# DSA's cost entry 40.0 to 74.0 in the emission mix of a two-layer decoder kernel

## Chip, core and metric

The kernel runs on one core of a Trainium2 chip. The metric is the device time of one execution in microseconds (us). Engines are named as in the profile: PE is TensorE (matmuls), DVE VectorE, ACT ScalarE, POOL GpSimd, SP SyncE.

## What is computed

Two decoder layers on 512 tokens of width 1024. Each layer normalises the input, projects it, runs four mixers of width 256 side by side (HGRN2, DSA, NSA, mLSTM), projects their joined output back, adds a cross-attention over 256 memory rows, and ends in a feed-forward block. Only the index branch of DSA matters closely here:

```python
topk = min(DSA_TOPK_MAX, l_ // 4)                     # 128
def block(bi):                                        # 128 queries at a time
    ...
    rel = jax.nn.relu(jnp.einsum('bthd,bsd->bhts', iqb, ik))   # 8 index heads
    # weighted sum over the heads, causal mask, then the 128 best keys of each query;
    # attention of that query runs over these keys alone
```

So for each block of 128 queries (tb = 0 to 3) there are eight score products, a weighted sum, and a choice of the 128 largest keys. Block 0 needs no choice.

## The kernel before

**Stages.** Each layer has a first stage (DSA's index branch, NSA, mLSTM and the projections that feed them, `weave` at L1535), a second stage (HGRN2, called hg, DSA's attention, output projection, cross-attention) and the feed-forward block. In time: first and second stage of layer 1 lie in 0 to 523 us, feed-forward to 872, layer 2's stages to 1390, its feed-forward to the end.

**What sets the order.** The program is one static instruction list for each engine, and an engine works its list in order. Generators emit work and `yield` a cost after each piece; `mix` takes the generator whose emitted cost, divided by its total in the table COST (L200), is smallest. What was emitted earlier has precedence in the scheduler that then lays out the lists. Weight projections are emitted early and with high precedence through `first()`.

**The index branch.** `dsa` (L607) yields 4.0, then for tb = 1, 2, 3 eight times 0.7 from `index` and sixteen times 0.4 + 0.25 tb from `select`: 64 in all. `index(tb)` makes eight score matmuls (L644), evicts them on ACT (`rel`, L646) and adds them into `iacc` on DVE (L649 to L653). `select(tb)` runs 16 rounds on DVE, each a MAX8 (L661) and a MATCH_REPLACE8 with its MATCH_VALUE_LOAD (L662), and then writes the mask (`dmask`, L665). The width of a round is 128 (tb + 1): 256, 384, 512 columns.

**What stands behind it.** `hg_space` (L737) follows `dsa` in the same chain and closes the index branch's pool; `hg_in` (L743), last of the other chain, waits in emission until that is done, since the tiles `h_v` and `h_g` take that pool's place. `h_v` is a projection with the tokens on the partitions: 48 matmuls (L304 to L306, 128x256) for two blocks, into two PSUM banks `acc`, evicted on ACT at L450. Two more blocks follow, then h_g and the output projection. These weight matmuls need nothing from the mixers and fill PE while it would wait; they are called filler here.

**Names in the first stage.** mLSTM works head after head: 12 matmuls L1013 into the bank `mb`, the four evictions `m_p` (L1021, DVE), 20 matmuls L1030 (into `mb` again), then a normalisation `m_den` (L1034 on, DVE). L539, L517, L519, L458 and L570 are NSA's attention, L1126 its compressed branch. L678 to L688 prepare DSA's keys, L1246 transposes mLSTM's output, L821 are products of hg.

```python
def mix(self, *parts):
    parts = [[g, total, 0.0] for g, total in parts]
    while parts:
        p = min(parts, key=lambda p: p[2] / p[1])
        try:
            c = next(p[0]); p[2] += c
            yield c
```

```python
self.weave((self.chain(self.dsa(pd, pk), self.hg_space(index, right)), COST["dsa"]),
           (self.chain(self.nsa_in(pn), ...), COST["two"]))
```

Of the kernel before, what the change touches and what calls it, by code (L numbers as in the profile page):

```python
# [196 lines left out]
RAWS = 6  # L197

OUT_K = ((4, 5, 6, 7), (2, 3), (0, 1))
COST = {"dsa": 40.0, "nsa": 140.0, "ml": 41.0, "in": 78.0, "mlin": 100.0, "two": 225.0, "attn": 49.42, "hg": 92.2, "out": 21.47, "ahead": 1834.58}  # L200


class Kernel:
# [41 lines left out]
    def first(self):  # L245

        return ExitStack() if self.starting else self.tc.high_priority(offset=int(COST["ahead"]))

# [1248 lines left out]
    def run(self):  # L1497
        nc = self.nc
        late = ExitStack()
        for l in range(DEPTH):  # L1500
# [31 lines left out]
            for tb in range(TB):  # L1532
                with self.first():
                    nc.scalar.activation(self.d_idx[:, tb], acc[tb], AF.Copy, scale=self.rcol[:, tb:tb + 1])
            self.weave((self.chain(self.dsa(pd, pk), self.hg_space(index, right)), COST["dsa"]),  # L1535
                       (self.chain(self.nsa_in(pn),
                                   self.mix((self.nsa(pn), COST["nsa"]),
                                            (self.chain(self.ml_in(pm),
                                                        self.mix((self.ml(pm), COST["ml"]),
                                                                 (self.chain(self.ml_in2(pm), self.dsa_in2(pk), self.hg_in()), COST["in"]))),  # L1540
                                             COST["mlin"]))),
                        COST["two"]))
# [48 lines left out]
```

## Time and profile before

| what | value |
|---|---|
| time, median of 3 runs | 1744.96 us (1742.71 to 1750.66) |
| profiled execution | 1746.31 us, of which the profile's span is 1744.5 us |
| PE busy | 1660.6 us, 95% of the span |
| DVE busy | 917.5 us, 53% |
| POOL busy | 785.8 us, 45% |
| ACT busy | 721.2 us, 41% |
| mean granted TensorE clock | 0.93 of 2.4 GHz |

Busy shares are averages over stages. Matmuls overlap and their ends are modelled, so a PE that is busy all the time can still work at half of its clock: the granted clock must be read beside the busy time.

### The profile page before, as it was taken

What the parts mean: (1) busy time and instruction counts of PE and PEld (TensorE: products, weight loads), DVE (VectorE), ACT (ScalarE), POOL (GpSimd) and SP (SyncE); (2) the same over time, 40 slices, a digit from 0 to 9 for tenths busy, and PEclk for the clock granted to TensorE, in tenths of its full rate; (3) what the DMA queues carried; (4) which work ended last, traced back from release to release, by engine and by line L of the source; (5) the groups of instructions that cost most, each with busy time, mean ns of one, the idle gap of its engine ahead of it and who ended that gap; (6) DMA issues with size and microseconds to landing.
All of it is one profiled execution on the core that took longest, in us unless ns stands there. A gap on an engine that the chain in (4) does not pass through costs nothing.

```text
span 1744.5 us, 25169 instructions
## 1 busy us (share of the span) xinstructions
PE 1660.6 (95%) x9262; PEld 1377.2 (79%) x9262; DVE 917.5 (53%) x1760; ACT 721.2 (41%) x1525; POOL 785.8 (45%) x698
## 2 busy tenths in 40 slices
PE   7889996999899999999998899989998999999999
PEld 7868774878788888888897687779786888888887
DVE  5685578756764430443227935796658544214420
ACT  5455532245553322333345644413566533223321
POOL 6653332346714444444446523233565244444442
PEclk9989985699999999999999899856998999999999
DMA  5233111021503333333233312010232133333332
GB/s 167 80 98 84 55 39 62 23 69 46 161 13 98 97 88 101 96 97 95 87 106 86 113 51 69 25 55 25 80 94 83 43 91 94 89 101 97 92 102 66
DMA packets 83259, 140.40 MB, mean 80 GB/s; under 512 B 9528, under 2 KB 24632, under 8 KB 83136
## 3 DMA queue, kind: packets, MB, share of 16 engines
q1 hardware_dynamic: 80784, 133.81, 26.1%
q10 hardware_dynamic: 2032, 3.94, 0.7%
q8 instruction: 73, 1.20, 0.3%
q0 software_dynamic: 320, 1.05, 0.2%
q14 instruction: 50, 0.41, 0.1%
HBM read 134.55 MB, written 4.21 MB: 80 GB/s over the span
## 4 chain that ended last, share of the span: by engine, by line
PE 79%; DVE 12%; issue 3%; ACT 2%; DMA 2%; POOL 2%; SPq 0%; ACTq 0%; POOLq 0%; DVEq 0%
PE acc L294 13%; PE acc L295 12%; PE acc L296 12%; PE sc L295 5%; PE sc L296 5%; PE sc L294 5%; PE hb L821 3%; PE acc L304 3%; PE acc L305 3%; PE acc L306 2%; PE sc L517 2%; PE o L539 2%; PE mb L1030 2%; PE tp L458 1%; DMA wr<-in_wst 1%
## 5 line engine op out<-in xcount | busy, mean ns | idle before, releaser
L286 POOL TENSOR_TENSOR wl<-wr,wh 128x512 fp32r<-128x512 f32 (+5 forms) x504 | 629.7, 1257 | 736.6 <-ACT wh L285 717.8
L285 ACT ACTIVATE wh<-wr 128x512 fp32r<-128x512 f32 (+5 forms) x504 | 298.2, 597 | 505.8 <-PE acc L295 195.9
L294 PE MATMUL acc<-xh,wh 128*128 128x512 f32 (+1 forms) x704 | 274.8, 392 | 2.4 <-DVE xT L431 2.3
L296 PE MATMUL acc<-xh,wl 128*128 128x512 f32 (+1 forms) x704 | 273.7, 389 | 0.8 <-POOL wl L286 0.8
L295 PE MATMUL acc<-xl,wh 128*128 128x512 f32 (+1 forms) x704 | 274.0, 389 | 0.0
L431 DVE TENSOR_TENSOR xT<-acc,xT 128x512 f32<-128x512 f32 (+1 forms) x112 | 68.2, 612 | 231.4 <-PE acc L296 231.2
L294 PEld LDWEIGHTS acc<-xh,wh 128*128 128x128 f32 x704 | 132.9, 189 | 32.4 <-DVE xT L431 1.9
L296 PEld LDWEIGHTS acc<-xh,wl 128*128 128x128 f32 x704 | 133.1, 189 | 28.1 <-POOL wl L286 2.1
L295 PEld LDWEIGHTS acc<-xl,wh 128*128 128x128 f32 x704 | 133.2, 189 | 27.0 <-issue 0.4
L295 PE MATMUL sc<-xl,wh 128*128 128x512 f32 x352 | 139.6, 397 | 0.0
L304 PE MATMUL acc<-wh,xh 128*128 128x256 f32 (+2 forms) x480 | 139.0, 291 | 0.3 <-DVE xT L431 0.3
L296 PE MATMUL sc<-xh,wl 128*128 128x512 f32 x352 | 139.0, 395 | 0.0
L295 PE MATMUL acc<-f_gl,wh 128*128 128x512 f32 x352 | 138.3, 395 | 0.0
L294 PE MATMUL acc<-f_gh,wh 128*128 128x512 f32 x352 | 138.2, 395 | 0.0
L296 PE MATMUL acc<-f_gh,wl 128*128 128x512 f32 x352 | 138.2, 394 | 0.0
L294 PE MATMUL sc<-xh,wh 128*128 128x512 f32 x352 | 138.1, 393 | 0.0
L305 PE MATMUL acc<-wl,xh 128*128 128x256 f32 (+2 forms) x480 | 137.9, 289 | 0.0
L306 PE MATMUL acc<-wh,xl 128*128 128x256 f32 (+2 forms) x480 | 137.1, 287 | 0.0
L1450 DVE SCALAR_TENSOR_TENSOR f_b<-sc,R 128x512 f32<-128x512 f32 x44 | 30.4, 690 | 127.7 <-PE sc L296 127.7
L304 PEld LDWEIGHTS acc<-wh,xh 128*128 128x128 f32 x480 | 91.6, 191 | 3.0 <-issue 1.2
L305 PEld LDWEIGHTS acc<-wl,xh 128*128 128x128 f32 x480 | 91.7, 191 | 1.5 <-issue 0.5
L306 PEld LDWEIGHTS acc<-wh,xl 128*128 128x128 f32 x480 | 91.7, 191 | 0.2 <-issue 0.2
(405 smaller groups left out, 3151.9 us busy)
## 6 DMA issues: line engine op xcount, KB each, us to landing
wr<-in_wst SPq DMA_DIRECT2D x384, 256.0 KB, 2.6
wr<-in_wst SPq DMA_DIRECT2D x48, 128.0 KB, 2.2
wr<-in_wst SPq DMA_DIRECT2D x32, 192.0 KB, 2.4
wr<-in_wst SPq DMA_DIRECT2D x16, 262.0 KB, 2.7
wr<-in_wst SPq DMA_DIRECT2D x16, 148.0 KB, 2.4
wr<-in_wst SPq DMA_DIRECT2D x8, 264.0 KB, 2.8
m_Mb<-m_dram ACTq DMA_DIRECT2D x8, 256.0 KB, 3.6
xT<-in_xT SPq DMA_DIRECT2D x8, 256.0 KB, 4.5
```

Of the source, the lines that this page charges most:

```text
L285: nc.scalar.activation(hi, raw, AF.Copy)
L286: nc.gpsimd.tensor_tensor(lo, raw, hi.bitcast(FT), op=OP.subtract)
L294: self.nc.tensor.matmul(acc, wh, xh, start=(j == 0), stop=False)
L295: self.nc.tensor.matmul(acc, wh, xl, start=False, stop=False)
L296: self.nc.tensor.matmul(acc, wl, xh, start=False, stop=(j == n - 1))
L304: self.nc.tensor.matmul(acc, xh[:, s], wh, start=(first and j == 0), stop=False)
L305: self.nc.tensor.matmul(acc, xh[:, s], wl, start=False, stop=False)
L306: self.nc.tensor.matmul(acc, xl[:, s], wh, start=False, stop=(last and j == n - 1))
L431: self.nc.vector.tensor_add(self.xT[c][:, cols], acc, self.xT[c][:, cols])
L517: nc.tensor.matmul(sc[:, e], q[j][:, h0 + e], job["kst"][:, :n], start=(j == 0), stop=False, skip_group_check=True)
L539: nc.tensor.matmul(o[64 * e:64 * e + 64, hp], job["v"](sb), job["pT"][2 * hp + e][:, sb * 128:sb * 128 + 128], start=(sb == 0), stop=(sb = ...
L821: nc.tensor.matmul(sc[s0:s1, b + t0:b + t1], kk[po:po + 64, b + s0:b + s1], qq[po:po + 64, b + t0:b + t1], start=True, stop=True)
```

## The change

One number of the table COST is another; no generator, instruction or tile is added or removed.

```diff
-COST = {"dsa": 40.0, "nsa": 140.0, "ml": 41.0, ..., "two": 225.0, ...}
+COST = {"dsa": 74.0, "nsa": 140.0, "ml": 41.0, ..., "two": 225.0, ...}
```

The yields of `dsa` sum to 64. With 40 its progress passes 1 before its end, and it reaches 64/40 = 1.60: the rest of `mix`, whose progress ends at about 1, is emitted to its end before the last index block and its choice. With 74 its end lies at 64/74 = 0.87, so 13% of the other parts' list is emitted after it.

The DVE list in the first layer, where the choice for tb = 3 starts (`m_2942` and `m_2244` are the eight maxima of a round, `mo_106` mLSTM's output, `kv` DSA's keys, `m_p` mLSTM's evictions). Before:

```order
L1042 TENSOR_REDUCE m_den<-m_sq 128x4
L661 MAX m_2942<-iacc 128x8
L312 TENSOR_SCALAR rs_ms<-m_den 128x4
L662 MATCH_REPLACE iacc<-m_2942,iacc 128x512
L312 TENSOR_SCALAR rs_ms<-dt 128x4
L661 MAX m_2942<-iacc 128x8
L316 TENSOR_TENSOR mo_106<-mo_106,m_den 128x4x64
L662 MATCH_REPLACE iacc<-m_2942,iacc 128x512
L316 TENSOR_TENSOR mo_106<-mo_106,m_tok 128x4x64
L661 MAX m_2942<-iacc 128x8
L316 TENSOR_TENSOR kv<-dt,d_st_3273 128x512
```

After:

```order
L1021 SCALAR_TENSOR_TENSOR m_p_2862<-mb,m_d 128x512
L653 SCALAR_TENSOR_TENSOR iacc<-rel,d_idx,iacc 128x512
L661 MAX m_2244<-iacc 128x8
L316 TENSOR_TENSOR mo_105<-o,spread 128x2x128
L521 TENSOR_REDUCE stat<-sc 128x1
L662 MATCH_REPLACE iacc<-m_2244,iacc 128x512
L1021 SCALAR_TENSOR_TENSOR m_p_2871<-mb,m_d 128x384
L661 MAX m_2244<-iacc 128x8
L1021 SCALAR_TENSOR_TENSOR m_p_2934<-mb,m_d 128x256
L662 MATCH_REPLACE iacc<-m_2244,iacc 128x512
L1021 SCALAR_TENSOR_TENSOR m_p_2968<-mb,m_d 128x128
L661 MAX m_2244<-iacc 128x8
```

The 16 rounds stood behind mLSTM's last head, among the preparation of keys and hg. They now stand among the evictions of mLSTM's last two heads.

The ACT list around the eviction of the first two blocks of `h_v` (`qh` and `P` belong to DSA's attention, `m_d` and `m_sq` to mLSTM, `ckvsq` to DSA's keys). Before:

```order
L525 ACTIVATE P,stat<-sc,stat 128x256 x2
L338 ACTIVATE sq<-d_q 128x256
L490 ACTIVATE qh<-dt 128x512
L450 ACTIVATE h_v<-acc,r_2765 128x256 x2
L1278 ACTIVATE memacc<-memT 128x256
L450 ACTIVATE h_v<-acc,r_2765 128x256
```

After:

```order
L1019 ACTIVATE m_d<-m_Mb,m_cols 128x128
L678 ACTIVATE ckvsq<-d_ckv 128x512
L1017 ACTIVATE m_d<-m_Md,m_cols 128x128
L450 ACTIVATE h_v<-acc,r_2873 128x256 x2
L1041 ACTIVATE m_sq<-mo_106 128x256
L1278 ACTIVATE memacc<-memT 128x256
L450 ACTIVATE h_v<-acc,r_2873 128x256
```

The eviction stood behind two blocks of DSA's attention; it now stands before the last normalisation of mLSTM.

The PE list in the first layer, where the last index scores stand (`iqs` are the index queries, `PT`, `n_tok`, `n_kst` belong to NSA's attention). Before:

```order
L458 MATMUL dt<-kc,iqs 96x128 x4
L1013 MATMUL mb<-m_hi_2645,m_hi_2697 128x256
L1013 MATMUL mb<-m_lo,m_hi_2697 128x256
L1013 MATMUL mb<-m_hi_2645,m_lo 128x256
L458 MATMUL dt<-kc,iqs 96x128 x4
L1013 MATMUL mb<-m_hi_2645,m_hi_2697 128x128
L1013 MATMUL mb<-m_lo,m_hi_2697 128x128
L1013 MATMUL mb<-m_hi_2645,m_lo 128x128
L644 MATMUL dt<-ikT,iqT 128x512
```

After:

```order
L306 MATMUL acc<-wh,xl 128x256
L458 MATMUL tp<-kc,P 128x128 x4
L539 MATMUL o<-PT,n_tok 64x128
L517 MATMUL sc<-n_kst_846,qh 128x512
L517 MATMUL sc<-n_kst_846,ql 128x512
L519 LDWEIGHTS identb
L519 MATMUL sc<-trib,identb 128x128
L1013 MATMUL mb<-m_hi_2749,m_lo 128x512
L644 MATMUL dt<-ikT,iqT 128x512
L539 MATMUL o<-PT,n_tok 64x128 x7
```

The eight L644 of tb = 3 stood behind the last weight matmul of the stage, between mLSTM's matmuls. They now lie spread over the weight matmuls and NSA's attention; the eighth, shown here, comes after most of them. The second layer's lists move in the same way.

## Rows read from the trace of the kernel before

**Rows 1.** The page's second part: granted clock in 40 slices.
```profile
PEclk9989985699999999999999899856998999999999
```

**Rows 2.** Windows of layer 1; busy us and instructions by engine, clock, DMA.
```profile
core 0: us, PE busy (x) PEld busy (x) DVE busy (x) ACT busy (x) POOL busy (x), PEclk, DMA share, GB/s
...
100.00:130.00 30.00, 22.42 (x139) 18.06 (x140) 28.09 (x65) 17.07 (x44) 14.85 (x14) 0.72 0.30 89
...
210.00:247.00 37.00, 36.78 (x241) 29.45 (x239) 32.91 (x77) 13.46 (x26) 12.99 (x10) 1.00 0.20 53
...
430.00:470.00 40.00, 37.10 (x213) 31.10 (x212) 30.60 (x42) 24.86 (x53) 29.80 (x31) 1.00 0.51 154
470.00:523.00 53.00, 47.77 (x348) 40.45 (x348) 37.53 (x83) 31.11 (x78) 12.28 (x11) 0.94 0.12 37
```

**Rows 3.** Windows, same columns: from keys' preparation to the next filler, layers 1 and 2.
```profile
280.40:334.90 54.50, 39.57 (x177) 34.16 (x177) 52.53 (x132) 10.34 (x28) 20.18 (x29) 0.50 0.15 50
...
1144.10:1203.20 59.10, 53.85 (x253) 47.62 (x253) 58.20 (x142) 7.77 (x23) 22.73 (x36) 0.50 0.12 41
```

**Rows 4.** Windows of 10 us inside and behind the layer 1 stretch.
```profile
260.00:270.00 10.00, 9.08 (x24) 5.63 (x24) 6.33 (x16) 5.04 (x12) 1.02 (x1) 0.50 0.00 0
...
280.00:290.00 10.00, 2.08 (x8) 1.78 (x8) 9.97 (x29) 0.62 (x2) 4.47 (x11) 0.50 0.61 202
...
340.00:350.00 10.00, 10.00 (x85) 9.41 (x85) 0.18 (x1) 5.47 (x13) 5.08 (x4) 1.00 0.38 107
```

**Rows 5.** Timeline of PE: start, duration, line, operation, [idle before, releaser].
```profile
247.64 0.50 PE L1013 MATMUL mb<-m_hi,m_hi 64*128 64x512 f32 x1 [0.86 <-ACT m_hi L980]
...
272.11 4.53 PE L1030 MATMUL mb<-m_v,m_p 128*128 128x65 f32 x20
...
278.53 1.09 PE L1246 MATMUL tp<-kc,mo 128*128 128x128 f32 x4
...
334.86 0.58 PE L304 MATMUL acc<-wh,xh 128*128 128x256 f32 x1
...
1111.89 0.49 PE L1013 MATMUL mb<-m_hi,m_hi 64*128 64x512 f32 x1 [0.71 <-ACT m_hi L980]
...
1203.19 0.58 PE L304 MATMUL acc<-wh,xh 128*128 128x256 f32 x1
```

**Rows 6.** Timeline of DVE: mLSTM's last two heads.
```profile
249.86 0.68 DVE L1021 SCALAR_TENSOR_TENSOR m_p<-mb,m_d 128x512 f32<-128x512 f32 x1
...
262.15 0.16 DVE L1034 COPY m_den<-mb 128x4 f32<-128x4 f32 x1 [2.95 <-PE mb L1030]
...
265.81 0.69 DVE L1021 SCALAR_TENSOR_TENSOR m_p<-mb,m_d 128x512 f32<-128x512 f32 x1 [0.15 <-PE mb L1013]
...
271.77 0.28 DVE L1021 SCALAR_TENSOR_TENSOR m_p<-mb,m_d 128x128 f32<-128x128 f32 x1
```

**Rows 7.** Timeline of DVE: one round at 512 columns, and the last mask.
```profile
284.45 0.68 DVE L661 MAX8 m<-iacc 128x8 f32<-128x512 f32 x1
...
285.96 0.69 DVE L661 MAX8 m<-iacc 128x8 f32<-128x512 f32 x1
...
331.88 0.42 DVE L665 TENSOR_SCALAR dmask<-iacc 128x512 bf16<-128x512 f32 x1
```

**Rows 8.** Groups by line on PE in 247 to 279: busy us, mean ns | idle before.
```profile
L644 PE MATMUL dt<-ikT,iqT 96*128 96x512 f32 x8 | 6.3, 788 | 0.7 <-ACT rel L646 0.7
L458 PE MATMUL dt<-kc,iqs 128*96 128x128 f32 x8 | 2.2, 427 | 0.0
```

**Rows 9.** Timeline of ACT: eviction of the first two blocks of h_v.
```profile
332.44 0.83 ACT L450 ACTIVATE h_v<-acc,r 128x256 f32<-128x256 f32 x2
```

**Rows 10.** Timeline of DVE: one round at 256 columns (tb = 1).
```profile
126.15 0.43 DVE L661 MAX8 m<-iacc 128x8 f32<-128x256 f32 x1
...
127.13 0.43 DVE L661 MAX8 m<-iacc 128x8 f32<-128x256 f32 x1
```

More of the change, by code (lines that the diff above doesn't have):

```diff
@@ L199 @@
 OUT_K = ((4, 5, 6, 7), (2, 3), (0, 1))
-COST = {"dsa": 40.0, "nsa": 140.0, "ml": 41.0, "in": 78.0, "mlin": 100.0, "two": 225.0, "attn": 49.42, "hg": 92.2, "out": 21.47, "ahead": 1834.58}
+COST = {"dsa": 74.0, "nsa": 140.0, "ml": 41.0, "in": 78.0, "mlin": 100.0, "two": 225.0, "attn": 49.42, "hg": 92.2, "out": 21.47, "ahead": 1834.58}
 class Kernel:
```

## Prediction

> **What bounds the kernel now.** I read the granted clock in slices first, because PE is busy nearly everywhere and its busy share hides where it is slow. The clock is at full speed except in two places, one in each layer [rows 1]. Windows then show what these places are. In layer 1 the clock stands at 0.50, that is 1.2 of 2.4 GHz, from about 250 us on, and is 1.00 again in 340 to 350 [rows 4]. PE's timeline gives the ends: its last weight matmuls are over when mLSTM's next head starts at 247.64, and the next filler starts at 334.86; in layer 2 these are 1111.89 and 1203.19 [rows 5]. So each layer has a hole of some 87 to 91 us.
>
> The hole has two parts. First come mLSTM's last two heads, a chain that goes back and forth between PE and DVE, until L1246 at 278.53 [rows 5, 6]. Then DVE bounds: in 280.4 to 334.9 it is busy 52.53 of 54.5 us, in layer 2 58.20 of 59.1 [rows 3], with the 16 rounds of tb = 3 among the preparation of hg and of DSA's attention; at its worst PE has 2.08 us of work in 10 [rows 4]. It ends with the last mask at 331.88 [rows 7] and the eviction of `h_v` at 332.44 [rows 9], which frees the two banks that the filler needs. This eviction waits by its place in ACT's list, behind DSA's attention, not for anything of its own. The feed-forward blocks, two fifths of the span, run at full clock [rows 1] and are not touched.
>
> **What the change moves, layer 1.** No work is added; I price when the filler resumes (T) and how much PE work of the old hole is then still to be done.
>
> Start of the hole. The eight L644 and eight transposes of tb = 3 come out of the hole (6.3 + 2.2 us there, at half clock [rows 8]) and lie among dense matmuls, where I price them at half of that: 4.2 us. The rounds of tb = 1 and 2 stand 25 and about 50 places earlier in DVE's list. At 100 to 130 DVE is busy 28.09 of 30 us already and PE idles 7.6 us [rows 2]; rounds put ahead of what PE waits for there cost it time. The trace of before cannot show how much. Bounds are 0 (the later stretch 210 to 247 shows PE busy 36.78 of 37 us while the rounds of tb = 2 run on a DVE busy 32.91 [rows 2], so rounds can be hidden) and 10, the idle time there now and a third more. I take 5, nearer to the DVE-bound row, since the moved rounds come towards that stretch. The hole so starts at 247.6 + 4.2 + 5 = 256.8.
>
> Length of the hole. In DVE's new list the rounds lie among the last two heads. A round at 512 columns takes 1.51 us from MAX8 to MAX8 [rows 7]; 16 make 24. Step by step: the third head needs 12.3 us from its first `m_p` to its `m_den` (249.86 to 262.15 [rows 6]), and the five rounds put in there (7.5 us) fit into DVE's idle time beside it. Up to the fourth head's first `m_p` the chain took 3.7 us (262.15 to 265.81), now with three rounds in the same queue: 3.7 + 4.5 = 8.2. Through its four `m_p` it took 6.0 (265.81 to 271.77), with three and a half rounds, 5.3 us, between: 9, between 6.0 and 11.3. Then L1030, 4.5 us from 272.11, and L681 with L1246, some 3 us until 279.6 [rows 5]: 7.5. Sum 12.3 + 8.2 + 9 + 7.5 = 37. The last four rounds and the mask run beside this end. `h_v` is evicted by then, as it stands behind the last `m_d`, and the filler starts at T = 256.8 + 37 = 293.8 instead of 334.9: 41.1 us earlier.
>
> What is late next. In the old hole PE did hg and DSA attention work in 280.4 to 334.9, 39.57 us busy at clock 0.50 [rows 3]. In the new order that comes after T, mixed with filler, and I price it at full clock: 19.8 us. What is left is 41.1 - 19.8 = 21.3 us.
>
> **Layer 2** by the same steps: the hole starts 4.2 + 5 later than 1111.9, T = 1111.9 + 9.2 + 37 = 1158.1, which is 45.1 before 1203.2; the work to be done later is 53.85/2 = 26.9; left 18.2. Together 39.5 us.
>
> **What takes some of it back.** The filler (144 matmuls for the rest of `h_v` and for h_g, then the output projection) is used up while hg's chain and DSA's attention still run, and at the end of the second stage PE then waits for them. Now, 430 to 523 has 8.1 us of PE idle time [rows 2]. I bound the added wait by 0 and 12 us in each layer and take 5, somewhat over half of what is lost there now, so 10 for both.
>
> Sum: 39.5 - 10 = 29.5 us. The profiled execution took 1746.3 (span 1744.5 and 1.8 around it), which gives 1716.8; that execution stands 1.3 above the median of the runs, so I name 1716.
>
> **The clock in the new hole.** In 260 to 270 PE shows 9.08 of 10 us busy and still the granted clock is 0.50 [rows 4]; it comes back only in the filler. So I price the new hole at half clock, as the heads' rows are. The Trainium skill (TensorE: Matmul & The Clock Gate, section Why this matters for your kernels) says that idle gaps between bursts of matmuls bring the clock back to half rate. The trace agrees in the fall at 250, and by it the order after, which puts NSA's attention and the scores among dense matmuls, might keep the clock up to the end of the heads; that is rival A.
>
> **Rivals.** A, the clock holds, or is lost late. PE's part of the chain is then half as long: L1030's 4.5 us and about 7 us of the third head's 12.3 shrink, T comes 5.6 us earlier in each layer, and with the queue's loss at the front at 0 another 5: 21 us more, 1695. For it speaks that NSA's attention, at full clock before 247, now stands beside the third head; against it that rows of a nearly busy PE stay at 0.50 [rows 4].
>
> B, the rounds do not overlap the heads. If DVE's order makes each wait for the other, the hole is 32 us of heads (247.6 to 279.6) and 24 of rounds, 56 in place of 37. That takes 19 from each layer: 39.5 - 38 - up to 10, about 1745 to 1755, no change. For it: DVE and PE each work in order, and a head's eviction now waits behind up to two rounds. Against it: the rounds need nothing from PE once `iacc` is summed.
>
> C, slower: the earlier rounds of tb = 1 and 2 hold up the front. Place: DVE's queue at 100 to 150 and 970 to 1010, ahead of NSA's scores and mLSTM's `m_p`. Price: a round at 256 columns takes 0.98 us [rows 10], one at 384 about 1.25, halfway to the 1.51 of 512; 16 of each are 36 us in a layer, and if PE waits for all of them, with 5 already counted, the loss is 62 us: 1779. The change turns slower from about 20 us of front loss in each layer on. For it: PE stands at clock 0.72 in 100 to 130 for want of DVE [rows 2]. Against it: the same rounds are hidden in 210 to 247.
>
> D, the change has no effect, if `h_v` were held by the last mask as now. Its new place in ACT's list speaks against it; then T would be about 296 anyway.
>
> **How the numbers follow.** Forecast with its bounds 1700 to 1735: 0.56. A, about 1695: 0.13. B and D, 1736 to 1755: 0.17. C, over 1755, centre 1779: 0.14. The range that should hold 8 in 10 reaches from 1692 (A with a little more) to 1750 (most of B); C stays outside. A measurement here tells about 0.5%, 8.7 us, from no change: faster by more holds for the forecast, A and a small part of B, 0.71; within it 0.15; slower 0.14.
>
> **What would show it.** Right: clock 0.50 from about 257 to 295 and from 1121 to 1160 and not until 335 and 1203; the first `h_v` eviction at about 285 to 294; the last mask near 295. The front's loss: mLSTM's last two heads start at 257 rather than 252 (no loss) or over 270 (C). The tail: PE idle time of 13 us rather than 8 before the feed-forward, which itself starts near 507. It would be wrong first if the rounds and the heads' evictions queue up on DVE (mask near 313: B), or if filler resumes early but PE falls to half clock again in hg's levels.

## The result, and where the time went

The changed kernel takes 1701.0 us (1697.2 to 1706.9, 4 runs) against 1744.3 for the kernel before: ratio 0.9748, 95% interval [0.9708, 0.9788], 43 us less. The forecast was 1716, 29 us less. So the sign and the place of the gain were forecast, and the gain is half as large again as the sum. Not all of it came by the forecast's way: the run with 66 below gains 29 us although it leaves the sixteen rounds of tb = 3 behind the heads.

The feed-forward block starts after everything that the change moves. Its first and last evictions (L1450) show what each layer gained; the view is the line's own, kernel before and kernel after, with the first and last start:

```profile
L1450 DVE SCALAR_TENSOR_TENSOR f_b<-sc,R x44: 678/691/692, 531.9 to 1679.2; 128x512 f32<-128x512 f32 x44
```
```profile
L1450 DVE SCALAR_TENSOR_TENSOR f_b<-sc,R x44: 680/691/692, 510.2 to 1636.4; 128x512 f32<-128x512 f32 x44
```

Layer 1 gains 21.7 us, both together 42.8, so layer 2 gains 21.1. The page after, its second part (granted clock in 40 slices), answers to [rows 1]: the two slices at 5 and 6 in each layer have become one at 7 (255 to 298 and 1106 to 1149 us; the other 7, at 936, is the front of layer 2, which had 8).

```profile
PEclk9989997999899999999999799979999999999999
```

The hole after, in windows (columns as in [rows 2]), answers to [rows 4]:

```profile
250.00:260.00 10.00, 7.44 (x72) 6.04 (x71) 9.49 (x28) 4.28 (x11) 0.71 (x1) 0.97 0.00 1
260.00:270.00 10.00, 6.58 (x18) 4.09 (x18) 9.87 (x24) 2.55 (x7) 1.02 (x1) 0.50 0.00 1
270.00:280.00 10.00, 7.80 (x38) 7.74 (x38) 8.18 (x23) 0.72 (x2) 1.92 (x2) 0.50 0.01 2
280.00:290.00 10.00, 10.00 (x87) 10.00 (x87) 1.02 (x4) 3.46 (x7) 5.69 (x12) 1.00 0.87 307
...
300.00:310.00 10.00, 7.03 (x21) 4.89 (x21) 8.88 (x11) 2.60 (x5) 7.24 (x6) 0.69 0.29 79
```

The clock is at half for some 20 us, where it was for 90, and DVE is full there. What stands in the hole is seen on PE (answers to [rows 5]):

```profile
239.48 0.50 PE L1013 MATMUL mb<-m_hi,m_hi 64*128 64x512 f32 x1
...
243.25 0.50 PE L644 MATMUL dt<-ikT,iqT 96*128 96x512 f32 x1
243.68 0.98 PE L539 MATMUL o<-PT,n_tok 128*64 128x128 f32 x13
...
265.34 0.58 PE L1013 MATMUL mb<-m_hi,m_hi 64*128 64x256 f32 x1 [1.38 <-DVE m_p L1021]
...
268.65 4.53 PE L1030 MATMUL mb<-m_v,m_p 128*128 128x65 f32 x20 [0.69 <-DVE m_p L1021]
...
276.99 1.08 PE L1246 MATMUL tp<-kc,mo 128*128 128x128 f32 x4 [2.20 <-DVE mo L316]
277.72 0.56 PE L304 MATMUL acc<-wh,xh 128*128 128x256 f32 x1
```

and on DVE (answers to [rows 6, 7]):

```profile
243.53 0.68 DVE L1021 SCALAR_TENSOR_TENSOR m_p<-mb,m_d 128x512 f32<-128x512 f32 x1
...
254.29 0.14 DVE L1034 COPY m_den<-mb 128x4 f32<-128x4 f32 x1
...
260.56 0.68 DVE L1021 SCALAR_TENSOR_TENSOR m_p<-mb,m_d 128x512 f32<-128x512 f32 x1
...
268.31 0.28 DVE L1021 SCALAR_TENSOR_TENSOR m_p<-mb,m_d 128x128 f32<-128x128 f32 x1
...
276.08 0.43 DVE L665 TENSOR_SCALAR dmask<-iacc 128x512 bf16<-128x512 f32 x1
```

The filler is back at 277.7 instead of 334.9. `h_v` is evicted on ACT long before:

```profile
265.68 0.82 ACT L450 ACTIVATE h_v<-acc,r 128x256 f32<-128x256 f32 x2
```

So the two banks no longer hold the filler up; PE itself does, which comes to it only after the fourth head. Layer 2 looks alike: the first eviction of `h_v` starts at 1111.6 in place of 1200.6, and the filler is back at 1123.8 in place of 1203.2.

To see where time is lost I take, for a window, its length less PE's busy time times the granted clock: idle time, and the share of busy time that half clock wastes. It is rough (the differences in layer 1 sum to 29 us, and 21.7 were gained), but it tells the places. Layer 1, before, after, and two runs told below, each line from the windows of that kernel:

| window | before | after (74) | 85 | 130 |
|---|---|---|---|---|
| 60 to 130, front | 70 - 57.31 x 0.85 = 21.3 | 70 - 58.78 x 0.88 = 18.3 | 70 - 56.20 x 0.82 = 23.9 | 70 - 52.36 x 0.71 = 32.8 |
| 130 to 240 | 0.2 | 1.3 | 3.4 | 12.4 |
| 240 to 340, hole | 100 - 81.30 x 0.56 = 54.5 | 100 - 88.09 x 0.86 = 24.2 | 100 - 91.14 x 0.92 = 16.2 | 100 - 97.65 x 1.00 = 2.4 |
| 340 to 430 | 0 | 2.9 | 11.5 | 9.4 |

### The profile page after: what moved, and what is told of

It is laid out like the page before. It is cut to its first block, busy times and chain, and to the rows that moved or that the text cites. A ratio compares the mean times of both kernels' runs of the same rounds, so it can differ in the third digit from the quotient of the medians.

```text
span 1701.7 us, 25165 instructions
## 1 busy us (share of the span) xinstructions
PE 1619.9 (95%) x9255; PEld 1339.9 (79%) x9262; DVE 943.7 (55%) x1760; ACT 718.3 (42%) x1525; POOL 790.9 (46%) x698
## 4 chain that ended last, share of the span: by engine, by line
PE 77%; DVE 13%; issue 4%; ACT 2%; DMA 2%; POOL 2%; SPq 0%; POOLq 0%; ACTq 0%; DVEq 0%
PE acc L296 13%; PE acc L294 13%; PE acc L295 13%; PE sc L295 5%; PE sc L296 5%; PE sc L294 5%; PE hb L821 3%; PE acc L304 3%; PE acc L305 2%; PE acc L306 2%; DVE iacc L662 2%; DVE m L661 2%; PE o L539 2%; PE sc L517 1%; PE tp L458 1%
## 5 line engine op out<-in xcount | busy, mean ns | idle before, releaser
L1450 DVE SCALAR_TENSOR_TENSOR f_b<-sc,R 128x512 f32<-128x512 f32 x44 | 30.4, 690 | 127.7 <-PE sc L296 127.7
```

## Experiments

The theory at first (P): the gain comes from the place of the sixteen rounds of tb = 3 and of `h_v` against mLSTM's last two heads. Rivals: S, it comes from the scores spread among dense matmuls and other moves ahead of the hole; C, earlier rounds hold up the front. Four kernels, each only another number in COST (the fourth: 74 in layer 1, 40 in layer 2).

**66**

```diff
-COST = {"dsa": 40.0, ...}
+COST = {"dsa": 66.0, ...}
```

> COST dsa 66: the index scores of tb = 3 are spread over the weight matmuls almost as with 74, but the sixteen rounds of tb = 3 and the first eviction of h_v stand behind mLSTM's heads as with 40. Theory P (the place of the rounds and of h_v against the last two heads makes the gain): within 10 us of before, 1735 to 1750. Rival S (spreading the scores among dense matmuls and the other moves at the front make it): most of the 43 us, 1700 to 1715.

Measured 1718.3 us (before, measured beside it, 1747.3; ratio 0.984 [0.982, 0.986]): 29 us of gain without the move of the rounds of tb = 3. Neither expectation holds: P lies 17 us too high, S 3 us too low. Theory P as I had put it falls. Timeline of PE and ACT of this kernel:

```profile
237.55 0.44 PE L1013 MATMUL mb<-m_hi,m_hi 64*128 64x384 f32 x1
...
250.81 0.50 PE L1013 MATMUL mb<-m_hi,m_hi 64*128 64x512 f32 x1
...
258.36 2.45 PE L1030 MATMUL mb<-m_v,m_p 128*128 128x65 f32 x20 [0.45 <-DVE m_p L1021]
...
280.89 3.09 PE L821 MATMUL hb<-h_q,h_k 64*128 64x128 f32 x16 [10.67 <-DVE h_q L806]
```
```profile
319.53 0.82 ACT L450 ACTIVATE h_v<-acc,r 128x256 f32<-128x256 f32 x2
```

Its windows:

```profile
250.00:260.00 10.00, 9.23 (x79) 7.04 (x78) 5.60 (x15) 6.38 (x17) 1.02 (x1) 1.00 0.00 0
...
270.00:280.00 10.00, 0.22 (x2) 0.00 (x0) 8.32 (x23) 1.68 (x3) 1.21 (x2) 0.50 0.66 225
```

The DVE-bound second part of the hole is still there, at half clock, and `h_v` comes at its end (319.5, 12.9 earlier than in [rows 9]). But the first part is gone: mLSTM's last two heads run from 234.5 (the third head's first L1013, just ahead of the rows shown) to 261 at full clock, with NSA's last attention, which before had ended on PE ahead of them (its last L570 at 245.2), now between their matmuls. L1030's twenty matmuls take 2.45 us in place of the 4.53 of [rows 5]. So the hole had two causes with two prices: the heads alone at half clock, and the rounds ahead of the filler. With 66 the first is mended, with 74 the second too, at the price that the fourth head now waits for rounds. The prices differ by layer: by the L1450 marks (520.5 and 1650.3) 66 gains 11.4 us in layer 1 and 17.5 in layer 2, where 74 gains 21.7 and 21.1. Which of the moves made with 66 keeps the clock up over the heads (scores out of them, NSA's attention into them, the early rounds) is read from these rows; no run moves one of them alone.

**85 and 130**

> COST dsa 85: the rounds start about 25 places earlier on DVE than with 74, and h_v's first eviction stands ahead of the fourth head's evictions, so filler lies among the heads. Theory P: the 16 us still lost in 245 to 280 and in the same place of layer 2 shrink by a third or more, 1688 to 1700. Rival C (earlier rounds hold up the front): at or above 1705.

> COST dsa 130: all rounds of all three blocks stand ahead of the third head's evictions. Theory P: the hole at the heads is about as short as with 85. Rival C: DVE's bound stretch at 60 to 130 and 910 to 985, which loses 18 and 22 us with 74, loses 10 or more on top in each layer, and the time is 1715 or above. If the front takes the rounds without loss: 1688 to 1702.

85: 1700.4 us, the same as 74 within the intervals (ratio 0.973 [0.970, 0.975]); it lies 0.4 above the upper edge of what P expected and below what C did. 130: 1713.3 (0.980 [0.978, 0.983]), between the two expectations. The table above shows where: the hole goes on shrinking, from 24 to 16 to 2 us, as P has it; the front loses 5.6 us more with 85 than with 74, and 14.5 more with 130, where 130 to 240 loses 11 more besides, as rival C has it; and from 85 on a loss appears at 340 to 430 that I had not priced (below). Windows of the kernel with 130, front and hole:

```profile
60.00:130.00 70.00, 52.36 (x305) 43.48 (x304) 61.83 (x145) 32.36 (x81) 22.45 (x20) 0.71 0.18 50
...
240.00:340.00 100.00, 97.65 (x662) 78.35 (x660) 62.80 (x130) 47.08 (x107) 45.93 (x45) 1.00 0.23 71
```

So rival C exists, but needs earlier rounds than the change makes.

**74 in layer 1 alone**

```diff
-..., self.hg_space(index, right)), COST["dsa"]),
+..., self.hg_space(index, right)), (74.0 if l == 0 else 40.0)),
```

> COST dsa 74 in the first layer and 40 in the second. If the layers gain separately, the first keeps its 21.7 us: 1722 to 1724. If weights loaded ahead or another thing carries over from layer to layer, the time differs from 1723 by more than 6 us.

Measured 1725.5, 1.5 us above the narrow range expected, which counted from a before of 1744.3; the before measured beside it was 1747.3, so the gain is 21.8 us, half of the whole. The layers gain separately.

**Half the rounds of tb = 3**, in the kernel before and in the changed one:

```diff
-            for r in range(16):
+            for r in range(8 if tb == 3 else 16):
...
-                yield 0.4 + 0.25 * tb
+                yield (0.4 + 0.25 * tb) * (2 if tb == 3 else 1)
```

> The kernel before with 8 rounds in place of 16 for tb = 3, so its last mask keeps 64 keys in place of 128; the yields keep their sum. Theory R (the second part of the old hole is bound by DVE, whose rounds cost 1.5 us each there): 12 us less in each layer, 1718 to 1726. Rival (that part is bound by hg's and DSA's own chains at half clock): less than 5 us in each layer, 1735 to 1745.

> The changed kernel with 8 rounds for tb = 3 in the same way. Theory R (the rounds among mLSTM's last two heads now set the pace there: DVE is busy 27.5 of 30 us in 250 to 280): with 66, where no round stands there, the two heads took 10 us less, so 8 to 12 us less in each layer, 1677 to 1687. Rival (the heads' own chain at half clock sets the pace, the rounds only fill its gaps): within 3 us in each layer, 1695 to 1704.

Before: 1723.7, 22 us less (ratio 0.988 [0.984, 0.991]) for 8 rounds of 1.5 in each layer. By the L1450 marks (522.7 and 1656.2) it is 9.2 in layer 1 and 13.8 in layer 2, far over the rival's 5: theory R holds, DVE bound the second part of the old hole. After: 1686.8, 14 us less than 1701.0, between R and its rival. The layer 1 mark (L1450's first start) moves from 510.2 to 499.0, so there R's 8 to 12 us are seen; layer 2 keeps 7.6 (1617.6 against 1636.4 at the last start, less the 11.2). What set the pace in the new hole were mostly the rounds: PE's rows above wait for `m_p` that stands behind them.

**Rounds of tb = 1 and 2 late, those of tb = 3 early; and a step between 74 and 85.** The yields of each block were scaled and COST set to 100, so that the blocks end at chosen shares of the list:

```diff
+BLOCK = (0.0, 2.25, 0.90, 0.50)       # second kernel: 1.44, 1.05, 1.12
-                yield 0.7
+                yield 0.7 * BLOCK[tb]
-                yield 0.4 + 0.25 * tb
+                yield (0.4 + 0.25 * tb) * BLOCK[tb]
```

> Cost 100 and the yields of the three blocks scaled so that they end at 0.40, 0.58 and 0.70 of the list: the rounds of tb = 1 and 2 stand where they stood before the change (2 places off for tb = 1, 20 earlier for tb = 2), those of tb = 3 ten places behind the changed kernel's. If the front costs nothing with 74 (as the loss in 60 to 130 and 910 to 985 says, 18 and 22 us against 20 and 19): 1696 to 1706. If it costs 5 us in each layer, as the prediction took it: 1686 to 1694.

> Cost 100, the blocks end at 0.27, 0.48 and 0.75: the rounds of tb = 1 and 2 as with 74, those of tb = 3 a little earlier. If the loss at the heads falls with earlier rounds, as with 85, while the front stays that of 74 and the filler is not used up: 1688 to 1697. If what is saved at the heads comes back at 310 to 410 for want of filler, as with 85: 1698 to 1704.

The first took 1708.3 (0.979 [0.975, 0.983]), 2 us above its first expectation: nothing is won by putting the early rounds back. Alone this does not show that the front is free, since the rounds of tb = 3 stand ten places later too (`h_v` is evicted at 279.4). The loss in the front does: in 60 to 130 and 910 to 985 it is 17.3 and 17.4 us here, 18.3 and 21.5 with 74, 21.3 and 20.1 before, so the front costs at most some 4 us with 74, in layer 2. The second took 1719.6 (0.986 [0.982, 0.990]), outside both expectations and 19 us above its two neighbours 74 and 85. Its windows in the second stage show the place:

```profile
330.00:340.00 10.00, 9.46 (x55) 7.92 (x51) 8.69 (x20) 2.27 (x10) 2.73 (x4) 0.70 0.01 2
340.00:350.00 10.00, 10.00 (x49) 8.57 (x50) 6.22 (x14) 2.11 (x6) 3.90 (x5) 0.50 0.00 0
...
390.00:400.00 10.00, 10.00 (x73) 6.75 (x72) 3.74 (x7) 4.36 (x13) 4.54 (x6) 0.50 0.06 15
400.00:410.00 10.00, 9.62 (x93) 8.26 (x94) 5.16 (x12) 6.09 (x18) 3.25 (x5) 0.88 0.06 16
```

PE is busy almost without a break and the clock is at half for more than 65 us. The loss is in this layer: the first eviction of the feed-forward (there L1451) starts at 530.3, 20 us later than with 74, and the last at 1651.7, 15 later, so layer 2 loses nothing more. The timeline at its start (this kernel's lines stand one further down, so L822 is hg's L821):

```profile
331.33 1.16 PE L822 MATMUL hb<-h_qs,h_k 64*128 64x128 f32 x8
...
333.63 4.90 PE L822 MATMUL hb<-h_qs,h_ks 64*128 64x128 f32 x24
...
340.09 2.08 PE L822 MATMUL hb<-h_qs,h_ks 64*128 64x128 f32 x8
```

Here 24 and more of hg's products stand together with no weight matmul between. The filler had been taken earlier: it starts at 269.0, among the fourth head's matmuls, and its last weight matmul ahead of this stretch starts at 326.1; the next comes at 359.5. In the changed kernel the same products are interleaved with the output projection (128x512), and its windows from 310 to 420 show 0.97 to 1.00. That gave theory K: where hg's products stand long without weight matmuls, the granted clock falls although PE is busy. PE's lists then named other places: the longest such stretch is 10 us in layer 1 and 6.5 in layer 2 for 85 and for this kernel, under 2 and 4.8 for 74, under 2.5 in both for 70 and 72 (estimates from the order of the lists, priced at full-clock durations of the trace). The traces show some that are longer: from weight matmul to weight matmul 31.8 us in layer 1 and 13.6 in layer 2 for 85, 9.6 and 12.2 in layer 2 for 74, 4.6 for 72.

**72 and 70, chosen for that**

> COST dsa 72: the rounds of tb = 3 end six places later on DVE than with 74 in layer 1 and nine in layer 2, and no stretch of the second stage has more than 2.5 us of matmuls without a weight matmul among them (with 74 layer 2 has two, of 4 and 5 us). Theory K (in such stretches the granted clock falls): layer 2's 3 us lost in 1145 to 1270 go, the rest stays: 1695 to 1703. Without K: 1700 to 1706.

> COST dsa 70: like 72, with mLSTM's last two heads seven places nearer to the front of DVE's list and the first eviction of h_v five places later on ACT. Theory P and K: 1696 to 1705; between 66 (1718) and 74 (1701) if the place of the rounds acts step by step: 1705 to 1712.

1697.2 (1694.3 to 1699.7; 0.972 [0.970, 0.975]) and 1698.3 (0.973 [0.971, 0.976]). Both lie within what P and K expected, and 70 is not a step towards 66. But K's own point for 72, less loss in layer 2, is not seen: by the L1450 marks (504.0 and 1629.8) layer 2 gains 21.5 us, as with 74, and it is layer 1 that gains 6 more. 72 is 4 us under the changed kernel's median, but the intervals of 70, 72, 74 and 85 overlap: no version was shown to beat 74. The values within 70 to 74 are a plateau, and 66 with 1718 stands outside it.

**The gate projection late.** The changed kernel with the last line of `hg_in` moved to a generator at the head of the second stage's output chain:

```diff
-        yield from self.proj_tok("hgg", lambda tb: self.h_g[:, tb], 256, self.x)
+    def hg_gate(self):
+        yield from self.proj_tok("hgg", lambda tb: self.h_g[:, tb], 256, self.x)
...
-(self.chain(self.out_stage(0), ...), COST["out"])
+(self.chain(self.hg_gate(), self.out_stage(0), ...), COST["out"])
```

> The changed kernel with one part moved: the projection of h_g is emitted in the second stage, ahead of the output projection, in place of the end of the first. DVE's and ACT's lists up to h_v stay as they are; in the second stage 13 us (layer 1) and 10 us (layer 2) of hg's products then stand together without a weight matmul. Theory K (the clock falls in such a stretch although PE is busy, and comes back only with dense weight matmuls): the granted clock is 0.50 there, 10 to 40 us more in each layer, 1720 to 1780. Rival (a late filler only costs what PE then waits for): 1699 to 1708.

Measured 1721.2 (1717.9 to 1731.4; 0.987 [0.983, 0.992]), 20 us above 74: K's forecast at its lower edge, and far outside the rival's. The trace does not bear K out, though. Its windows in layer 1:

```profile
300.00:310.00 10.00, 6.37 (x40) 5.56 (x39) 9.01 (x17) 2.01 (x4) 6.69 (x7) 0.75 0.37 105
310.00:320.00 10.00, 10.00 (x47) 8.92 (x45) 5.78 (x13) 2.10 (x9) 2.48 (x4) 0.50 0.01 2
320.00:330.00 10.00, 10.00 (x50) 9.00 (x49) 8.68 (x23) 1.01 (x2) 3.72 (x5) 0.50 0.00 1
330.00:340.00 10.00, 9.38 (x58) 7.97 (x56) 9.90 (x27) 3.55 (x11) 4.49 (x6) 0.71 0.00 0
340.00:350.00 10.00, 9.88 (x127) 7.50 (x127) 8.68 (x20) 5.08 (x15) 5.05 (x8) 1.00 0.01 2
```
```profile
306.44 3.10 PE L823 MATMUL hb<-h_qs,h_k 64*128 64x128 f32 x16 [1.70 <-DVE h_aT L855]
...
335.93 1.71 PE L823 MATMUL hb<-h_qs,h_ks 64*128 64x128 f32 x16
```

The clock fell at about 305, while PE waited for DVE (1.45 and 1.70 us, the second shown here), not in the products that come after it. And it rose again at about 336, where sixteen products take 1.71 us in place of 3.10, although no weight matmul stands between 300.2 and 345.1: so it does not need weight matmuls to come back. Nor does the time go as K has it: the first eviction of the feed-forward (there L1452) starts at 508.1, 2 us earlier than with 74, so layer 1 lost nothing in spite of 30 us at half clock, and all of the loss is in layer 2 (the last at 1650.8 against 1636.4), where the clock is at 0.50 in 1170 to 1200.

**More work in those products.** The kernel of 1719.6 us with one dense matmul ahead of each group:

```diff
                 sc = self.psum("hb")
+                nc.tensor.matmul(sc, self.identb, self.d_masks[3], start=True, stop=True)
```

> The kernel of the run with blocks ending at 0.27, 0.48 and 0.75 (1719.6 us, clock 0.50 in 335 to 400) with one more matmul ahead of each group of hg's products, whose result is overwritten: identity by the last mask, 128 rows by 512 columns, some 0.23 us each, 32 in a layer, 15 us of PE work in all. The order of hg's products against the weights shifts with it. Theory K: the clock stays up between 335 and 400 and the time falls in spite of the added work, 1690 to 1710. Rival (the clock there follows something else): the added work comes on top, 1730 to 1740.

Median 1708.3, within K's expectation and 11 us less in spite of the added matmuls. But its three executions took 1727.5, 1708.3 and 1707.9 us with mean clocks 0.956, 0.969 and 0.969, and the one that was traced is the first: in it the clock still fell, to 0.50 in 340 to 370. Two executions speak for K, one against; and the order of the products shifted too. It shows no cause.

**What is left of K.** Not its rule. With 85, 56 of hg's products and some 50 other small matmuls stand in layer 2 from 1184.4 to 1198.0 without a weight matmul, and the clock stays at 1.00:

```profile
1185.00:1190.00 5.00, 4.65 (x39) 3.95 (x39) 5.00 (x10) 1.10 (x3) 3.42 (x4) 1.00 0.08 26
1190.00:1195.00 5.00, 5.00 (x44) 3.96 (x43) 4.80 (x16) 2.47 (x9) 1.53 (x2) 1.00 0.01 3
```

The two stretches of 74 in layer 2 (1209.6 to 1219.2 and 1230.6 to 1242.7) show 1.00 as well. What the traces do show: where the clock fell among such products, PE had waited shortly before, and then it stayed at 0.50 for 24 us (85), 30 (gate late), 41 (dense matmuls) and 68 (the kernel of 1719.6 us) with PE shown busy nearly all the time. Why some stretches keep the clock and others lose it, no run here shows.

## Why the prediction was right, and where its sum was off

**The bound.** Right: two holes at half clock, with DVE's rounds and the late filler in them, and they are where the gain came from (54 to 24 us in layer 1). The run with half the rounds in the kernel before confirms the DVE bound by 9.2 and 13.8 us. But that the first part of the hole, the heads at half clock, would go in part with the change was no part of the forecast's sum, which priced the heads at half clock (rival A had it); by the run with 66 more than half of the gain comes without the move of the last rounds.

**The start of the hole (256.8).** This step failed most. I had put the third head's first matmul there; it came at 239.5, and the last L644 at 243.25. Two terms were wrong. The front's loss, taken as 5 us between 0 and 10, was none in layer 1: 60 to 130 loses 18 us in place of 21. And I had priced the new order as the old with index work added ahead of the hole; in fact NSA's last attention, some 10 us of PE work from 243.68 on, went the other way, from ahead of the heads to beside them. The listed order showed this second move; I had used it for rival A only. That the clock does fall near 257, as forecast (it is at 0.97 in 250 to 260 and 0.50 after), is luck: by then the third head is through.

**The length (37).** Close: from the first `m_p` of the third head to the filler it is 243.53 to 277.72, 34.2 us. Step by step 10.8 for 12.3, 6.3 for 8.2, 7.8 for 9, and 9.4 from the last `m_p` for 7.5; the last is longer because the fourth head's output waits behind the last rounds (2.20 us of idle time at L1246). The agreement is in part luck too, since the third head's step ran at full clock and not at half, and since the sum counts from the first `m_p` (249.86 before) but starts from the first matmul (247.64), so 2.2 us are left out. T is 277.7 in place of 293.8, and the signs that were named come early with it: the first eviction of `h_v` at 265.7 for 285 to 294, the last mask at 276.1 for 295.

**The work that is left at T (19.8).** Right in size: PE's records before T differ between the kernels by 128 L821 and 48 smaller matmuls of DSA's keys and attention, and by no weight matmul (layer 1).

**What is taken back (5 in each layer).** Too small. T is 57.2 us earlier; less 19.8 that is 37.4, and 21.7 was gained: 15.7 us went after T. In the trace PE idles behind DVE at 300 to 310, where the output projection waits for its split operand (`xl`, L1242) in a DVE queue now full of hg's preparation, about 6 us of loss there, 3 more in 340 to 430, and some 1 more in 430 to 501. There, at the end of the second stage, the prediction had put it all; PE idles 7.8 us there, against 8.1 in 430 to 523 before. About 6 us I can't place. So two mis-sized terms, 16 us too late and 11 us too little taken back, partly cancel. Layer 2 shows the same: T is 57.7 us earlier (layer 1's gain taken off) where 45.1 was forecast, and of the 30.8 left after the 26.9 of later work 21.1 were gained, so 9.7 were taken back.

One thing in the trace ahead of that DVE queue was not foreseen. With its rounds done early, DVE stands still for 9 us, until a load of `in_levels` lands that only layer 1 has; before, it waited 1.6 us for it:

```profile
288.99 0.36 DVE L792 CAST lv<-lvf 128x384 uint8<-128x384 f32 x1 [8.98 <-DMA lvf<-in_levels]
```
```profile
303.96 0.79 PE L295 MATMUL acc<-xl,wh 128*128 128x512 f32 x1 [1.94 <-DVE xl L1242]
```

What an earlier load would save was not tried. It is not the whole of that loss: with 70, where DVE waits 0.4 us for the load, PE waits 3.2 us for `xl` in 290 to 330, against 2.7 with 74.

**Rival A (the clock holds, 1695).** Half true: the clock held until about 259, over the third head, and fell for the fourth. The time lies between the two, 6 us above A's and 15 below the forecast. A's price of 21 us beside the forecast was too high by the loss after T. The run with 66 shows a clock that holds over both heads. **Rival B** (no overlap) did not happen: 14 of the 16 rounds were read in 250 to 280, beside the heads. **Rival C** is seen in the front with 85 (5.6 us) and with 130 (14.5 us), not at 74. **Rival D** is out: `h_v` left its banks 10.4 us before the mask.

**The clock rule.** In the old hole PE had waited 0.86 and 0.62 us ahead of the fall, which came just before 250; in the run at 1719.6 us 0.19 and 0.35 us ahead of the fall at 334; with the gate late 1.45 and 1.70 us around 305. The Trainium skill (TensorE: Matmul & The Clock Gate, section Why this matters for your kernels) ties the fall to idle gaps between bursts. The traces agree in the direction, though each of these gaps is shorter than the one that the section names. It does not give what cost the run at 1719.6 us its time: there the clock stayed at 0.50 with PE busy 10.00 of 10 us. The measurement decides.

## What to carry to other kernels

When a wait on one engine is moved, list what else changes its neighbours: here a cost that leaves the last rounds where they were (66) brought 29 us, where 74 brought 43, with work that slid beside a slow chain. Filler is a stock: spent at one hole, it can be missing at the next. Read the granted clock beside busy time in every window, since a stretch can cost double with PE shown busy throughout.

## What the runs showed of the hardware

The clock stood at 1.2 GHz (0.50) for more than 65 us with PE shown busy 10.00 of 10 us, in a stretch of 64x128 products, small attention matmuls and scattered weight matmuls; it fell at about 334, as the 24 products from 333.63 on began, ahead of which PE had waited no longer than 0.35 us at a time since 328, and it came back between 400 and 410. Elsewhere it came back in such products without any weight matmul (gate late, at about 336), and stayed at 1.00 over 13.6 us of them (85, layer 2). With one kernel (dense matmuls added) executions of the same program differed by 19 us, by 0.956 and 0.969 in the mean clock. What exactly makes the clock fall in such a stretch stays open.
